# Splitting two blocks of the FFN activations where they are made instead of where they are multiplied

## The chip, the cores and the metric

The kernel runs on one core of one Trainium2 chip. The time is device microseconds of one launch: a median of 2877.29 us over three runs of the kernel before (2876.45 to 2877.64). One more execution was profiled, and every row below is from it. The engines are PE (TensorE, with PEld for its weight loads), DVE (VectorE), ACT (ScalarE), POOL (GpSimd) and SP (SyncE, which here only issues DMAs). Each engine works through its own instructions in order.

## The reference

Two layers, each a mixer (a gated delta net in layer 0, retention in layer 1) and a convolutional FFN, each followed by a residual sum and a layer norm. Sequence 1024, width 1024, FFN width 2816, all in float32. The change concerns the FFN alone:

```python
def conv_ffn(h, w_up, conv_w, conv_b, w_down):
    gate, up = jnp.split(h @ w_up, 2, axis=-1)
    gate = causal_dwconv(gate, conv_w) + conv_b
    return (jax.nn.silu(gate) * up) @ w_down

for i in range(DEPTH):
    ...
    y = conv_ffn(x * (1.0 + sc2) + sh2, ffn_up[i], ffn_conv_w[i], ffn_conv_b[i], ffn_down[i])
    x = layer_norm(DN_ALPHA * x + (1.0 + g2) * y, ln_g[i, 1], ln_b[i, 1])
```

Below, `o` is the product `silu(gate) * up`, the left factor of the down projection.

## The kernel before, in words

**Products in two parts.** A float32 factor x is written as a high part (x rounded to fp32r) and a low part (x minus the high part, again fp32r). A product of two such factors is three matmuls: low by high, high by low, high by high. `split` (L88 to L90) makes the parts: ACT copies x into the high part (L89), then DVE (or POOL, where a table says so) subtracts it from x (L90). So the subtraction waits for ACT each time.

**Blocks.** Both FFN projections use a Strassen-Winograd scheme on 2 by 2 blocks, with seven block products for eight. The left factor of the down projection is needed as seven blocks, in the order of `ABLK`: 11, 12, 22 (plain quarters of `o`) and S1 to S4 (sums and differences of quarters). Quarter 21 is used only inside the sums.

**The up stage** (`strassen`). There are 22 items of two units of 128 features (four quarters: two units by two halves of the sequence), taken as 11 pairs: a gate item and then an up item with the same pair number `fp`. An item is seven products of 12 matmuls of 512 columns (`wino`): a11, a12, s1, s2, s4, s3, a22, where s1 to s4 are weight sums that DVE forms into PSUM (L1350). Every weight block is split into a tile `wb` by ACT and DVE before PE can use it. An item's weights are two 512 KB loads, L1361 (a11, a12) and L1362 (a21, a22), into two buffers of the tag `wr`; a load waits until the last reader of the item before has left its buffer, which for L1362 is the split of a22. Results leave through `sink`: the gate's four quarters are convolved (`conv_q`: ACT L1734, DVE L1739 twice, ACT L1740), the up's four quarters are multiplied into `o` by DVE (L1762) in the order of quarters 0, 1, 3, 2. After quarter 3, block 22 is stored; after quarter 2, POOL forms S1, S2, S4 and S3 one after another (L1770; for pair 0 it is DVE), and each is stored. The stores (L1751) are SP's, 256 KB each, to a DRAM tensor `ad` with seven blocks a pair.

Besides that, the up stage carries other work a piece at a time: columns or rows of the condition's modulation (`bg_ada`, DVE L237 and L239; in layer 0 over nearly the whole stage, in layer 1 over its first pairs) and a gain of the residual on POOL (L411, L412).

**The down projection** (`proj_gen`). It has seven products p of 11 steps j; the left block of p is 11, 12, S1, S2, S4, S3, 22 in that order. A step is 12 matmuls. For a step, SP loads the left block from `ad` into `ar` (tag `qkv`, 20 buffers) and, three steps ahead, the weight block `Br` or `Bw`; both are split, into `ab` and `bb`. `ab` and `bb` take their buffers from a ring of the tags `wl`, `wr`, `wh` with two buffers each, two taken a step, so a buffer comes free when the step three before has ended. In layer 1 (`final`) a longer ring with the eight buffers of `hTb` is used, and the last six left blocks of product 22 lie in `hTb`; in layer 0 the last four lie in `qkv`. Between the steps, DVE finishes earlier products (`f1` to `f7`, `finish`, `norm`). In layer 0 the eight blocks of the next input are also built during the S3 product; in layer 1 the rows are normalised and written to the output.

**What sets the order.** The kernel is traced in the order of the code. A scheduler that runs a timeline of its own then orders each engine's instructions and hands out the buffers; `after(...)` adds an order on one engine. On the chip that order is fixed: an instruction that waits holds up all behind it on its engine.

The names that count below: `store` and `up_start` (L1750 to L1774), `ops` (L1481), `ablk_of` (L1425), and the tag `t2`, three buffers of 128 by 512, which the up stage uses for one copy an item (L1389).

Of the kernel before, what the change touches and what calls it, by code (L numbers as in the profile page):

```python
# [9 lines left out]
F32 = mybir.dt.float32  # L10
# [5 lines left out]
P = 128  # L16
# [3 lines left out]
HALF = 512  # L20
# [4 lines left out]
NF = F // P  # L25
HP = 3000
ABLK = ("11", "12", "22", "S1", "S2", "S3", "S4")
ALPHA = 4.0 ** 0.25
BAL = {"r11": 0, "r12": 0, "r22": 0, "rS1": 0, "rS2": 0, "rS3": 0, "rS4": 0, "rw21": 0, "rwT1": 0, "rwT2": 0, "rwT3": 0, "rwT4": 0, "rn": 0, "rh": 1, "011": 0, "012": 0, "022": 0, "0S1": 0, "0S2": 0, "0S3": 0, "0S4": 0, "0w21": 0, "0wT1": 0, "0wT2": 0, "0wT3": 0, "0wT4": 0, "0n": 1, "0h": 0, "f11": 0, "f12": 0, "f22": 0, "fS1": 0, "fS2": 0, "fS3": 0, "fS4": 0, "fw21": 0, "fwT1": 0, "fwT2": 0, "fwT3": 0, "fwT4": 0, "fn": 1, "fh": 0, "gw": 99, "gh": 0, "gn": 3, "b1": 0, "b2": 0, "b3": 0, "b4": 0, "bT": 0, "ba": 0, "rw11": 0, "rw22": 0, "0w11": 0, "0w22": 0, "fw11": 0, "fw22": 0}
LN_EPS = 1e-5  # L30
# [3 lines left out]
def trunk_kernel(ctx: ExitStack, tc, A):  # L34
# [53 lines left out]
    def split(dst_h, dst_l, src, eng=dve):  # L88
        anchor["sp"] = act.activation(dst_h, src, AF.Copy)  # L89
        eng.tensor_tensor(dst_l, src, dst_h, ALU.subtract)  # L90
# [1339 lines left out]
            return raw  # L1430
        return ablk

    def proj_gen(nj, ablk, wsrc, slots, xsrc, G, final, ln_next, tag, ltags, dst, key, mm=pe.matmul, gate=None):
        bal = {nm: BAL[ltags[4] + nm] for nm in ABLK + ("w11", "w21", "w22", "wT1", "wT2", "wT3", "wT4", "n", "h")}
        pa = [tl("aux", [P, 2, HALF], name="pa") for _ in range(4)]
        p1 = [pa[t // 2][:, t % 2] for t in range(4)]
# [27 lines left out]
        def bblk(bn, j):  # L1464
            if bn in ("11", "22"):
                return {"11": C, "22": X}[bn][j]
            if bn == "21":
                return R[bn, j]
            if bn == "T1":
                dve.tensor_tensor(C[j], R[bn, j], C[j], ALU.subtract)  # L1470
                return C[j]
            if bn == "T2":
                dve.tensor_tensor(C[j], X[j], C[j], ALU.subtract)
                return C[j]
            x, y = (R[bn, j], C[j]) if bn == "T4" else (C[j], R[bn, j])
            dve.tensor_tensor(R[bn, j], x, y, ALU.subtract)
            return R[bn, j]
# [1 line left out]
        nst = [0]  # L1479

        def ops(an, bn, j, early):  # L1481
            ra, rb = ablk(an, j), bblk(bn, j)
            n = nst[0]
            nst[0] += 1
            last = an == "22"
            ring = ("wl", "wr", "wh")
            at = ltags[0] if last and j >= nj - ltags[3] else ("wl", "hTb", "wr")[n % 3] if early else ring[2 * n % 3]
            wt = ltags[1] if last and j >= nj - ltags[2] else ("wh", "hTb", "hTb")[n % 3] if early else ring[(2 * n + 1) % 3]
            a = two(at, F32R, "ab")
            split(a[0], a[1], ra, pool if j < bal[an] else dve)  # L1490
            w = two(wt, F32R, "bb")
            split(w[0], w[1], rb, pool if j < bal["w" + bn] else dve)
            return a, w
# [188 lines left out]
    def layer_tail(i, mix, wout, xsrc, x_mid, x_out, ln_next, final):  # L1682
# [24 lines left out]
        cw = vcol(f"ffn_conv{i}")  # L1707
        cb = vcol(f"ffn_convb{i}")
        ad = dr.tile([NF // 2, 7, P, HALF], F32, tag=f"ad{i}", name=f"ad{i}")
        up = A["ffn_up"][i]  # L1710

        late = []

        def pair_items(fp):
            g, o = [], {}

            def gate_start():
                g.extend(tl("lane", [P, D], name="g") for _ in range(2))

                def gate(q, a, b):  # L1720
                    dst = g[q // 2][:, hs(q % 2)]
                    if b is None:
                        act.activation(dst, a, AF.Copy)
                    else:
                        dve.tensor_tensor(dst, a, b, ALU.add)
                return gate

            def conv_q(q):
                f, hf = 2 * fp + q // 2, q % 2
                gv = g[q // 2]  # L1730
                w = cw[:, 3 * f:3 * f + 3]
                t = tl("qkv", [P, HALF], name="o")
                with after("sp") if fp == 0 else nullcontext():
                    act.activation(t, gv[:, hs(hf)], AF.Copy, scale=w[:, 2:3])  # L1734
                for j in (1, 2):
                    c0 = HALF if hf else j
                    c1 = HALF * (hf + 1)
                    tv = t[:, c0 - HALF * hf:]
                    dve.scalar_tensor_tensor(tv, gv[:, c0 - j:c1 - j], w[:, 2 - j:3 - j], tv, ALU.mult, ALU.add)  # L1739
                act.activation(t, t, AF.Silu, bias=cb[:, f:f + 1])  # L1740
                o[q] = t

            def conv():
                for q in (1, 3, 0, 2) if fp == 0 else range(4):
                    if fp < 2:
                        late.append(lambda q=q: conv_q(q))
                    else:
                        conv_q(q)

            def store(nm, q):  # L1750
                sp.dma_start(ad[fp, ABLK.index(nm)], o[q])  # L1751

            def up_start():
                seen = []

                def gated(q, a, b):
                    while q not in o:
                        late.pop(0)()
                    c = a
                    if b is not None:  # L1760
                        dve.tensor_tensor(c, a, b, ALU.add)
                    dve.tensor_tensor(o[q], o[q], c, ALU.mult)  # L1762
                    if q != 1:
                        store({0: "11", 2: "12", 3: "22"}[q], q)
                    seen.append(q)
                    if len(seen) == 4:
                        for d, x, y, op, nm in ((1, 1, 3, ALU.add, "S1"), (0, 1, 0, ALU.subtract, "S2"),
                                                (2, 2, 0, ALU.subtract, "S4"), (3, 3, 0, ALU.subtract, "S3")):
                            def one(d=d, x=x, y=y, op=op, nm=nm):
                                (dve if fp == 0 else pool).tensor_tensor(o[d], o[x], o[y], op)  # L1770
                                store(nm, d)
                            if fp == 0:
                                late.append(one)
                            else:  # L1774
                                one()
                return gated

            return [(up[4 * fp], up[4 * fp + 2], gate_start, conv), (up[4 * fp + 1], up[4 * fp + 3], up_start, None)]
# [5 lines left out]
        if not final:  # L1784
            wnext_up.append(A["ret_wg"][2])
        gb2 = gain_rows(3, ("mid", i), "hTb") if final else None
        return proj_st(proj_gen(NF // 2, ablk_of(ad, "qkv"), A["ffn_down"][i], slots, xg[i + 1], rows[i, 5],
                       (gb2, x_out) if final else None, ln_next, "hTb", ("hTb", "hTa", 8, 6, "f") if final else ("qkv", "hTa", 8, 4, "0"), x_out, ("out", i)))

    g1 = two("auh", F32, "g1")  # L1790
    for nh in range(2):
# [384 lines left out]
```

## Time and profile before

| | |
|---|---|
| median of three runs | 2877.29 us |
| the profiled execution | 2872.01 us, its span 2870.2 us |
| granted TensorE clock | 0.994 |
| PE, PEld busy | 97%, 79% of the span |
| DVE, ACT, POOL busy | 76%, 45%, 17% of the span |
| DMA | 465.30 MB, a mean of 162 GB/s |
| stores `ad<-o`, loads `ar<-ad` | 154 each of 256 KB, 2.3 us and 4.7 us to landing (median) |

PE leaves the up stage at 1157.8 us in layer 0 and at 2644.5 us in layer 1; the down projections follow it. Their matmuls end near 1380 us and at 2855.97 us.

In a row of grouped instructions stand the line, the engine, the operation, out<-in by the program's names, the shape, the count, then the busy time and the mean of one in ns, then the idle time of the engine just before them and what ended it. In a row of the timeline stand the start, the duration, the engine, the line and the tiles, and in brackets the idle time before it with its releaser. In a row of windows stand the window, its length, each engine's busy time and count, the granted clock, the DMA engines' busy share and their GB/s. Matmuls are pipelined: one of 512 columns is shown with some 390 ns, and they start 0.23 us apart.

### The profile page before, as it was taken

What the parts mean: (1) busy time and instruction counts of PE and PEld (TensorE: products, weight loads), DVE (VectorE), ACT (ScalarE), POOL (GpSimd) and SP (SyncE); (2) the same over time, 40 slices, a digit from 0 to 9 for tenths busy, and PEclk for the clock granted to TensorE, in tenths of its full rate; (3) what the DMA queues carried; (4) which work ended last, traced back from release to release, by engine and by line L of the source; (5) the groups of instructions that cost most, each with busy time, mean ns of one, the idle gap of its engine ahead of it and who ended that gap; (6) DMA issues with size and microseconds to landing.
All of it is one profiled execution on the core that took longest, in us unless ns stands there. A gap on an engine that the chain in (4) does not pass through costs nothing.

```text
span 2870.2 us, 38920 instructions
## 1 busy us (share of the span) xinstructions
PE 2783.2 (97%) x13594; PEld 2276.5 (79%) x13594; DVE 2180.0 (76%) x3874; ACT 1296.7 (45%) x2387; POOL 486.9 (17%) x513
## 2 busy tenths in 40 slices
PE   8999999999999999999999999999999999999997
PEld 6778878887788878887888887777777788888886
DVE  6787778676788888778687656666788887777869
ACT  4664465344644444545433342222344644445443
POOL 0311321000023222000000002343201033322001
PEclk9999999999999999999999999999999999999999
DMA  7233242174255554945343354665754253444843
GB/s 279 85 99 122 92 133 96 64 246 153 99 180 172 195 182 167 337 133 172 129 147 131 116 198 156 198 208 155 258 203 147 74 194 132 143 139 164 319 148 118
DMA packets 252884, 465.30 MB, mean 162 GB/s; under 512 B 24144, under 2 KB 77776, under 8 KB 252688
## 3 DMA queue, kind: packets, MB, share of 16 engines
q1 hardware_dynamic: 218560, 408.02, 42.8%
q10 hardware_dynamic: 31488, 46.15, 4.4%
q0 software_dynamic: 2640, 8.65, 0.8%
q8 instruction: 107, 1.75, 0.2%
q14 instruction: 89, 0.73, 0.1%
HBM read 346.86 MB, written 115.87 MB: 161 GB/s over the span
## 4 chain that ended last, share of the span: by engine, by line
PE 60%; DVE 20%; DMA 8%; ACT 5%; issue 5%; POOL 1%; SPq 0%; ACTq 0%; DVEq 0%; POOLq 0%
PE acc L716 11%; PE acc L1296 5%; PE acc L1591 5%; PE sc L716 4%; PE acc L110 4%; PE acc L111 4%; PE acc L112 4%; PE sc L1296 3%; PE mm L716 2%; DVE o L1739 2%; DVE wb L90 2%; DMA mvw<-in_ada_w 2%; DMA wr<-in_ffn_up 2%; DVE mm L1350 2%; DVE ada L239 2%
## 5 line engine op out<-in xcount | busy, mean ns | idle before, releaser
L716 PE MATMUL acc<-hT,wh 128*128 128x512 f32 x960 | 298.3, 392 | 0.0
L1591 PE MATMUL acc<-bb,ab 128*128 128x512 f32 x984 | 230.9, 393 | 5.6 <-DVE bb L90 2.4
L89 ACT ACTIVATE ab<-ar 128x512 fp32r<-128x512 f32 x210 | 131.1, 630 | 218.9 <-PE mm L303 53.6
L1591 PEld LDWEIGHTS acc<-bb,ab 128*128 128x128 f32 x984 | 184.3, 189 | 47.3 <-DVE bb L90 3.2
L716 PEld LDWEIGHTS acc<-hT,wh 128*128 128x128 f32 x960 | 181.6, 189 | 35.3
L1296 PE MATMUL acc<-T,wb 128*128 128x512 f32 x840 | 202.0, 389 | 0.4 <-DVE wb L90 0.4
L89 ACT ACTIVATE wb<-mm 128x512 fp32r<-128x512 f32 x216 | 124.4, 597 | 167.3 <-DVE mm L1350 152.2
L90 DVE TENSOR_TENSOR ab<-ar,ab 128x512 fp32r<-128x512 f32 x210 | 145.8, 702 | 71.2 <-ACT ab L89 70.9
L716 PE MATMUL acc<-hT,wl 128*128 128x512 f32 x480 | 196.1, 409 | 2.5 <-ACT sq L509 2.5
L1296 PEld LDWEIGHTS acc<-T,wb 128*128 128x128 f32 x840 | 157.5, 188 | 33.8 <-ACT o L1740 1.2
L90 DVE TENSOR_TENSOR wl<-wr,wh 128x1024 fp32r<-128x1024 f32 x98 | 122.5, 1250 | 74.3 <-ACT wh L89 73.8
L89 ACT ACTIVATE wh<-wr 128x1024 fp32r<-128x1024 f32 x98 | 103.8, 1060 | 137.9 <-PE acc L716 54.3
L90 DVE TENSOR_TENSOR wb<-wr,wb 128x512 fp32r<-128x512 f32 x162 | 116.3, 719 | 64.2 <-ACT wb L89 64.1
L1770 POOL TENSOR_TENSOR o<-o 128x512 f32<-128x512 f32 x80 | 112.3, 1412 | 267.4 <-ACT pc L1366 173.1
L1739 DVE SCALAR_TENSOR_TENSOR o<-g,vc,o 128x512 f32<-128x512 f32 (+2 forms) x176 | 147.1, 845 | 8.6 <-ACT o L1734 7.3
L90 DVE TENSOR_TENSOR wb<-mm,wb 128x512 fp32r<-128x512 f32 x216 | 144.4, 681 | 7.4 <-ACT wb L89 7.4
L89 ACT ACTIVATE wb<-wr 128x512 fp32r<-128x512 f32 x162 | 101.1, 626 | 93.8 <-PE acc L1296 27.1
L1350 DVE TENSOR_TENSOR mm<-wr 128x512 f32<-128x512 f32 x108 | 85.7, 794 | 69.9 <-DMA wr<-in_ffn_up 56.8
L716 PE MATMUL acc<-wh,hT 128*128 128x512 f32 x384 | 134.8, 413 | 2.1 <-DVE vv L90 2.1
L1366 ACT ACTIVATE pc<-acc 128x512 f32<-128x512 f32 x143 | 84.4, 590 | 108.6 <-PE acc L1296 63.2
L239 DVE SCALAR_TENSOR_TENSOR ada<-mvw,e,ada 128x512 f32<-128x512 f32 x140 | 105.4, 753 | 26.6 <-DMA mvw<-in_ada_w 26.3
L110 PE MATMUL acc<-T,wb 128*128 128x512 f32 x292 | 114.4, 392 | 3.5 <-DVE wb L90 3.4
(675 smaller groups left out, 7348.1 us busy)
## 6 DMA issues: line engine op xcount, KB each, us to landing
wr<-in_ffn_up SPq DMA_DIRECT2D x92, 512.0 KB, 3.9
mvw<-in_ada_w SPq DMA_DIRECT2D x80, 512.0 KB, 4.4
ad<-o SPq DMA_DIRECT2D x154, 256.0 KB, 2.3
ar<-ad SPq DMA_DIRECT2D x154, 256.0 KB, 4.7
Br<-in_ffn_down SPq DMA_DIRECT2D x88, 256.0 KB, 5.2
wr<-in_ret_wv SPq DMA_DIRECT2D x32, 512.0 KB, 3.6
ar<-od SPq DMA_DIRECT2D x56, 256.0 KB, 5.0
wr<-in_gdn_wqkv SPq DMA_DIRECT2D x24, 512.0 KB, 3.5
```

Of the source, the lines that this page charges most:

```text
L89: anchor["sp"] = act.activation(dst_h, src, AF.Copy)
L90: eng.tensor_tensor(dst_l, src, dst_h, ALU.subtract)
L110: mm(acc, wl[:, k], hl[0], start=first, stop=False)
L111: mm(acc, wh[:, k], hl[1], start=False, stop=False)
L112: mm(acc, wh[:, k], hl[0], start=False, stop=last)
L239: dve.scalar_tensor_tensor(a, wr[:, kk], e[:, k:k + 1], a, ALU.mult, ALU.add)
L716: pq(pe.matmul(out, lhsT, rhs, start=start, stop=stop), cost or COST[out.shape[-1]])
L1296: return pe.matmul(*a, skip_group_check=True, **kw)
L1350: dve.tensor_tensor(t, x, y, op)
L1591: return pe.matmul(*args, skip_group_check=True, **kw)
L1739: dve.scalar_tensor_tensor(tv, gv[:, c0 - j:c1 - j], w[:, 2 - j:3 - j], tv, ALU.mult, ALU.add)
L1770: (dve if fp == 0 else pool).tensor_tensor(o[d], o[x], o[y], op)
```

## The change

For blocks 22 and S3 of both layers, `store` makes the two parts at once: ACT copies the block into a high part, DVE subtracts for a low part, both in tiles of the tag `t2`, and SP stores both to a new DRAM tensor `ah` in place of the one store to `ad`. In the down projection, the steps of products S3 and 22 load the two parts straight into the ring buffer `ab`, in two loads, and do not split the left block. The other five blocks are as before, and so is every matmul.

Per layer there are 22 such blocks, 44 in all: 44 splits (an ACT copy and a DVE subtraction) move from the down projection to the up stage, 44 stores of 256 KB become 88, and 44 loads become 88.

```diff
+HL = ("22", "S3")
...
-    def proj_gen(nj, ablk, wsrc, slots, xsrc, G, final, ln_next, tag, ltags, dst, key, mm=pe.matmul, gate=None):
+    def proj_gen(nj, ablk, wsrc, slots, xsrc, G, final, ln_next, tag, ltags, dst, key, mm=pe.matmul, gate=None, hlblk=None):
...
         def ops(an, bn, j, early):
-            ra, rb = ablk(an, j), bblk(bn, j)
+            pre = hlblk is not None and an in HL
+            ra, rb = None if pre else ablk(an, j), bblk(bn, j)
...
             a = two(at, F32R, "ab")
-            split(a[0], a[1], ra, pool if j < bal[an] else dve)
+            if pre:
+                for i in range(2):
+                    anchor["w"] = anchor["a"] = sp.dma_start(a[i].bitcast(F32), hlblk[j, HL.index(an), i])
+            else:
+                split(a[0], a[1], ra, pool if j < bal[an] else dve)
...
         ad = dr.tile([NF // 2, 7, P, HALF], F32, tag=f"ad{i}", name=f"ad{i}")
+        ah = dr.tile([NF // 2, 2, 2, P, HALF], F32, tag=f"ah{i}", name=f"ah{i}")
...
             def store(nm, q):
-                sp.dma_start(ad[fp, ABLK.index(nm)], o[q])
+                if nm not in HL:
+                    sp.dma_start(ad[fp, ABLK.index(nm)], o[q])
+                    return
+                hl = [tl("t2", [P, HALF], F32R, name="oh") for _ in range(2)]
+                act.activation(hl[0], o[q], AF.Copy)
+                dve.tensor_tensor(hl[1], o[q], hl[0], ALU.subtract)
+                for i in range(2):
+                    sp.dma_start(ah[fp, HL.index(nm), i], hl[i].bitcast(F32))
```

The call of `proj_gen` in `layer_tail` passes `hlblk=ah`; the retention's output projection does not, and is unchanged.

2 lines of the change are left out of this document (1 added, 1 removed).

## The prediction

> **What bounds the kernel now.** I read the totals first, then windows by stage, then the waits of a stage, then the timelines of its engines where a wait sits.
>
> ```profile
> PE 2783.2 (97%) x13594; PEld 2276.5 (79%) x13594; DVE 2180.0 (76%) x3874; ACT 1296.7 (45%) x2387; POOL 486.9 (17%) x513
> 787.00:1142.50 355.50, 351.63 (x1553) 287.39 (x1552) 300.08 (x462) 168.91 (x338) 104.64 (x84) 1.00 0.54 183
> 2290.00:2606.00 316.00, 315.48 (x1384) 259.26 (x1384) 247.52 (x365) 145.50 (x246) 98.89 (x79) 1.00 0.44 148
> ...
> 1320.00:1338.00 18.00, 18.00 (x84) 14.81 (x84) 15.91 (x36) 15.04 (x24) 2.63 (x3) 1.00 0.87 304
> ...
> 2820.00:2857.00 37.00, 35.07 (x153) 28.05 (x151) 37.00 (x72) 11.51 (x20) 6.38 (x4) 1.00 0.15 57
> 2857.00:2870.20 13.20, 0.00 (x0) 0.00 (x0) 9.98 (x22) 1.92 (x3) 3.05 (x2) 0.61 0.41 159
> ```
>
> The first row is the page's, the others are windows: layer 0's up stage (nine pairs of 39.5 us), layer 1's (eight), the middle of layer 0's S3 product, the kernel's last PE work, and what follows it. PE is the bound almost everywhere, so a split taken off DVE is worth nothing where PE is full. It counts in the last 50 us, where DVE is 100% busy and PE ends 14 us before the span does. And the up stage of layer 0 is not as free as 84% of DVE looks:
>
> ```profile
> PE acc L110 <- DVE wb L90: 3.4, 4, 1.2
> DVE mm L1350 <- DMA wr<-in_ffn_up: 24.2, 10, 3.6
> ```
>
> These are its waits by engine: PE already waits for DVE's weight splits, and DVE waits once a pair for a weight load. One pair, from one such stall to the next, on DVE, PE, POOL and SP:
>
> ```profile
> 904.86 1.29 DVE L1725 TENSOR_TENSOR g<-acc,pc 128x512 f32<-128x512 f32 x2 [1.27 <-ACT pc L1366]
> 906.07 1.28 DVE L90 TENSOR_TENSOR wb<-mm,wb 128x512 fp32r<-128x512 f32 x2
> 906.80 0.50 PE L110 MATMUL acc<-T,wb 128*128 128x512 f32 x1 [1.21 <-DVE wb L90]
> 924.61 5.62 POOL L1770 TENSOR_TENSOR o<-o 128x512 f32<-128x512 f32 x4
> 924.67 0.68 DVE L1762 TENSOR_TENSOR o<-o,sc 128x512 f32<-128x512 f32 x1
> 929.86 1.70 DVE L1739 SCALAR_TENSOR_TENSOR o<-g,vc,o 128x511 f32<-128x511 f32 x2 [0.24 <-ACT o L1734]
> 930.25 0.32 SPq L1751 DMA_DIRECT2D ad<-o  x1
> 931.48 0.69 DVE L90 TENSOR_TENSOR wb<-wr,wb 128x512 fp32r<-128x512 f32 x1
> 932.19 0.33 SPq L1362 DMA_DIRECT2D wr<-in_ffn_up  x1
> 933.41 0.69 DVE L90 TENSOR_TENSOR wb<-wr,wb 128x512 fp32r<-128x512 f32 x1 [1.25 <-ACT wb L89]
> 936.79 0.70 DVE L1350 TENSOR_TENSOR mm<-wr 128x512 f32<-128x512 f32 x1 [2.68 <-DMA wr<-in_ffn_up]
> ```
>
> Read it as a loop. From 904.86 to 932.16 DVE has hardly a gap. Its last job there, the split of a22, frees the weight buffer; SP issues the next load at 932.19; it lands at 936.8; then a chain of DVE and ACT work leads to the next weight split that PE needs, some 9 us later. In this pair and in about half of the others PE arrives first. So what is put on DVE between 905 and 932 moves the load, and PE's next stall, by its full length; what falls in the gaps at 932 to 937 is free.
>
> **The change, part by part.** All matmuls stay.
>
> *Up stage, layer 0.* Per pair two ACT copies, two DVE subtractions and two more stores are added.
>
> ```profile
> L90 DVE TENSOR_TENSOR wb<-mm,wb 128x512 fp32r<-128x512 f32 x8 | 5.3, 681 | 0.0
> L90 DVE TENSOR_TENSOR wb<-wr,wb 128x512 fp32r<-128x512 f32 x6 | 5.2, 870 | 1.3 <-ACT wb L89 1.3
> L89 ACT ACTIVATE ab<-ar 128x512 fp32r<-128x512 f32 x210 | 131.1, 630 | 218.9 <-PE mm L303 53.6 <-PE mm L1591 42.2 <-PE acc L1591 39.9
> ```
>
> The first two rows are DVE's splits in that pair: 0.68 us with one input in PSUM, 0.87 us with both in SBUF, as the new ones have them. Block 22's subtraction becomes ready with the multiplication just before 924, in the dense stretch: +0.8 us on the loop. S3's becomes ready when POOL's chain ends at 930.2, plus 0.63 us of ACT: about 931, within half a microsecond of a22's split. Behind that split it falls in the gap and costs nothing, except that its second store, if it stands ahead of L1362 on SP, delays the load by about 0.8 us; in front of it, 0.8 us to 1.5 us. So the load comes later by 0.8 to 2.3 us, and I take 1.1. Less the 0.3 us of slack that the pairs without a stall have, that is 0.8 us on nine pairs: **+7 us**, bounds 0 (DVE fits it all into gaps) and +18. ACT has room (169 us of 355). The extra 512 KB a pair is 13 GB/s on 183. The three `t2` buffers hold at most one copy and one pair of parts at a time, as the parts of 22 leave some 6 us before those of S3 are made; a store takes about 2 us.
>
> The Trainium skill speaks against the move here: page "SBUF — State Buffer", section "Who interferes with whom", says that a DVE instruction with two SBUF inputs contends with a GpSimd instruction that reads SBUF, and the later one waits until the earlier is done. The rows agree in kind (870 ns against 681) but not in full, since not each of them meets a POOL instruction. By the rule alone block 22's subtraction would wait for a rest of one of four POOL instructions; what that makes is the last rival.
>
> *Up stage, layer 1.* Less other work is mixed in, and the split that PE waits for is earlier:
>
> ```profile
> 2552.54 0.68 DVE L90 TENSOR_TENSOR wb<-mm,wb 128x512 fp32r<-128x512 f32 x1
> 2554.03 0.39 PE L110 MATMUL acc<-T,wb 128*128 128x512 f32 x1
> ```
>
> It ends 0.81 us before its use, and PE lost 0.5 us in 316. The same 1.1 us leaves 0.3 us in some pairs: **+1 us**, bounds 0 and +8.
>
> *Down projection, layer 1.*
>
> ```profile
> L90 DVE TENSOR_TENSOR ab<-ar,ab 128x512 fp32r<-128x512 f32 x18 | 12.0, 679 | 0.0
> ...
> 2841.55 0.96 PE L1591 MATMUL acc<-bb,ab 128*128 128x512 f32 x3 [0.66 <-DVE ab L90]
> 2842.76 3.47 PE L1591 MATMUL acc<-bb,ab 128*128 128x512 f32 x14 [0.24 <-DVE ab L90]
> 2843.78 12.19 PE L1591 MATMUL acc<-bb,ab 128*128 128x512 f32 x53
> ...
> 2846.83 0.69 DVE L1517 TENSOR_TENSOR acc<-acc,rowb 128x512 f32<-128x512 f32 x1
> 2857.02 0.69 DVE L1517 TENSOR_TENSOR acc<-acc,rowb 128x512 f32<-128x512 f32 x1
> 2866.36 0.69 DVE L1540 TENSOR_TENSOR xt<-xt,rowb 128x512 f32<-128x512 f32 x1
> ```
>
> The first row groups DVE's window 2796 to 2843: 18 left-block splits, and since two of 0.68 take 1.28 (row 906.07), one costs 0.60 in a full queue: 10.8 us, all of which go. DVE has no gap from there to the end. The last group of four accumulators is 72 matmuls at 0.23 us, so the first is done 12.3 us before PE's end at 2855.97, at 2843.7; DVE begins it at 2846.83, behind by 3.1 us. With the backlog gone it follows PE: each accumulator costs DVE 4.6 us (seven operations of 0.6 to 0.66 and small ones) against PE's 4.1, so the fourth starts at PE's end plus about 1 us less what PE gains (0.9 us of stalls), and its own chain with nothing of others in between takes some 6 us instead of the 10 from 2857.02 to 2867.05. That gives an end of DVE at about 2862.5: **-4.5 us**, bounds -6.5 and 0 (the scheduler keeps the order in which the accumulators' steps are mixed). The loads of the parts have a ring some six steps deep there and DMA is at 0.15.
>
> *Down projection, layer 0.* PE stalls near its end would go; the loads are the risk.
>
> ```profile
> 1317.49 0.63 ACT L89 ACTIVATE ab<-ar 128x512 fp32r<-128x512 f32 x1 [5.83 <-PE acc L1591]
> 1320.26 0.63 ACT L89 ACTIVATE ab<-ar 128x512 fp32r<-128x512 f32 x1 [1.61 <-PE acc L1591]
> ...
> 1354.36 0.66 PE L282 MATMUL mm<-cst,xt 128*128 128x128 f32 x4 [0.82 <-ACT t L284]
> 1355.56 1.65 PE L1591 MATMUL acc<-bb,ab 128*128 128x512 f32 x6 [0.54 <-DVE ab L90]
> ...
> DMA to landing us min/median/max: 2.6/3.4/6.3
> ```
>
> A left split starts when PE leaves the buffer, about every 2.75 us, two steps (5.5 us) ahead of use. Now two loads start there instead. The last row is the left loads of 1310 to 1342: 3.4 us for one, about 4.2 for two, in time; but 1320 to 1338 already moves 304 GB/s at a share of 0.87, thus 349 at most. Six or seven more loads of 262 KB make 401: 18 us of traffic become 20.7. The queue behind SP's waiting load is the weight load for three steps on, which has room. I take +2.5 for the DMA and -1.5 for the two stalls: **+1 us**, bounds -2 and +6.
>
> The sum is 7 + 1 - 4.5 + 1 = +4.5 us on the profiled execution's 2872.01 (span 2870.2 and 1.8 around it). The median of the runs is 5.3 us above that execution, and the difference goes onto the median: 2881.8, say **2882**. About 0.2% (5.8 us, so 2871.5 to 2883.0) is what a measurement can tell from no change; the forecast is a loss inside it.
>
> **The rivals.**
>
> *The up stage absorbs it* (not slower). The loop has 5.4 us of gaps a pair (1.27, 0.24, 1.25 and 2.68), and the scheduler may put both subtractions there. Against: block 22's is ready 8 us before the first gap of size and, traced earlier, goes first. Then 0 + 0 - 4.5 - 1.5 = -6: **2871**.
>
> *The in-order wait on POOL* (slower). If the scheduler's clock has POOL done earlier than the chip, S3's copy and subtraction stand well before a22's split, and ACT and DVE stand idle until POOL is done. It decides from the point where POOL's end at 930.2 plus ACT's 0.6 is later than DVE's turn; at 1.5 us a pair over the slack on nine pairs in layer 0 (+13.5) and 0.7 on eight in layer 1, whose slack is 0.8 (+5.6), the sum is 13.5 + 5.6 - 4.5 + 1 = +15.6: **2893**. Against: SP's order of stores and weight loads, laid down by the same scheduler, fits POOL's real end (S3's store at 930.25, 1.9 us ahead of L1362).
>
> *Loads late in layer 0's S3 and 22 products.* With a landing of 8 us for the pair, three steps take 11 us for 8.2, nine steps long: +8.4, less the 1.5: +7 in place of +1, the rest as in the sum: **2888**.
>
> *Contention with POOL.* Each of block 22's subtractions waits out one POOL instruction of 1.4 us: 1.4 us on nine pairs, about 0.5 on eight: +17 on the sum: **2898**. The page above has the rule; the 870 ns bear out a seventh of it.
>
> **How the numbers follow.** Forecast 0.42 (its own range 2877 to 2888; no change 0.25, slower 0.17); absorbed 0.30 (2867 to 2876; faster 0.17, no change 0.13); wait on POOL 0.16, late loads 0.08, contention 0.04, all slower. Together faster 0.17, no change 0.38, slower 0.45: the likeliest time is inside the bound, while the rivals' mass lies beyond it. The range 2870 to 2893 cuts off the ends of the first and the last of these.
>
> **What would show it.** In the new profile, layer 0's up pairs: PE's stalls for `wb` L90 at up items of 1 to 2 us in nearly each pair (right), none (absorbed), 3 us with DVE idle behind POOL (wait on POOL). Layer 1's last accumulator: L1517 within 1 us of PE's end and the span's end some 9 to 10 us after PE's instead of 14. Layer 0's S3 product: PE waiting for `ah` loads, or not. The forecast is wrong if the up stage's length in layer 0 moves by under 2 us or over 14, or if the end keeps its 14 us.

## The result and the profile after

The changed kernel took 2887.09 us (median of six runs, 2882.72 to 2893.75), the kernel before 2876.40 us beside it (2874.78 to 2877.64): ratio 1.0034, 95% interval 1.0023 to 1.0044, a loss of about 10 us. The forecast was 2882.0, with 2870 to 2893 as its range. The direction and the range hold. The size does not: I had forecast a loss of 4.5 us, inside what a measurement can tell from no change, and it is more than twice that and clear of it. Of the terms, two were missed, and the mechanisms of three rivals that I had given little chance are there, at part of their size.

The profiled execution of after is the slowest of its six (2893.75 us, span 2892.0), that of before lies below its median (2872.01). So I compare stage by stage. Windows of the kernel before, cut at the first and last matmul of layer 0's up and down stages, of layer 1's, and at the end of PE (columns: stretch, length, busy time of PE, PEld, DVE, ACT, POOL, clock, DMA share, GB/s):

```profile
763.00:1157.60 394.60, 389.24 (x1715) 317.40 (x1714) 334.38 (x516) 190.53 (x374) 104.64 (x84) 1.00 0.51 173
1157.80:1377.60 219.80, 216.00 (x958) 177.67 (x957) 172.92 (x285) 111.15 (x191) 11.94 (x11) 0.99 0.62 213
2257.70:2644.30 386.60, 385.08 (x1687) 315.69 (x1686) 306.59 (x456) 183.30 (x310) 106.10 (x84) 1.00 0.43 144
2644.50:2856.00 211.50, 210.53 (x925) 173.00 (x923) 174.88 (x293) 98.65 (x174) 15.94 (x10) 1.00 0.60 207
2856.00:2870.20 14.20, 0.00 (x0) 0.00 (x0) 10.98 (x24) 2.92 (x4) 3.05 (x2) 0.64 0.38 148
```

The same of the changed kernel:

```profile
770.30:1168.50 398.20, 389.88 (x1715) 317.37 (x1714) 348.36 (x536) 198.13 (x394) 108.56 (x84) 1.00 0.55 185
1168.70:1396.00 227.30, 218.53 (x958) 178.93 (x957) 159.38 (x261) 101.49 (x171) 9.70 (x10) 0.98 0.66 232
2278.30:2668.20 389.90, 386.01 (x1687) 315.47 (x1686) 322.34 (x476) 191.89 (x330) 107.69 (x84) 1.00 0.45 157
2668.40:2880.40 212.00, 210.88 (x925) 172.95 (x923) 167.35 (x279) 89.74 (x155) 14.78 (x10) 1.00 0.69 240
2880.40:2892.00 11.60, 0.03 (x1) 0.00 (x0) 7.70 (x18) 1.62 (x2) 1.84 (x2) 0.67 0.29 113
```

DVE's work moved as intended: 14 to 16 us more in each up stage, 13.5 and 7.5 us less in the down stages. The losses stand in layer 0: 3.6 us in its up stage and 7.5 us in its down stage, with 3.3 us in layer 1's up stage; the end gives back 2.6 us. The rest of the 21.8 us between the two spans (some 9.5 us) lies in stretches whose code the change doesn't touch. These together took between 1641 and 1656 us in the fourteen profiles of this study, so a difference of that size between two single executions says nothing.

### The profile page after: what moved, and what is told of

It is laid out like the page before. It is cut to its first block, busy times and chain, and to the rows that moved or that the text cites. A ratio compares the mean times of both kernels' runs of the same rounds, so it can differ in the third digit from the quotient of the medians.

```text
span 2892.0 us, 39009 instructions
## 1 busy us (share of the span) xinstructions
PE 2792.8 (97%) x13594; PEld 2281.5 (79%) x13594; DVE 2185.8 (76%) x3874; ACT 1293.2 (45%) x2387; POOL 485.1 (17%) x513
## 5 line engine op out<-in xcount | busy, mean ns | idle before, releaser
L91 DVE TENSOR_TENSOR ab<-ar,ab 128x512 fp32r<-128x512 f32 x166 | 118.5, 720 | 81.0 <-ACT ab L90 80.9
L90 ACT ACTIVATE ab<-ar 128x512 fp32r<-128x512 f32 x166 | 103.6, 628 | 162.0 <-PE mm L304 48.9
L1351 DVE TENSOR_TENSOR mm<-wr 128x512 f32<-128x512 f32 x108 | 78.7, 729 | 54.4 <-DMA wr<-in_ffn_up 41.6
L111 PE MATMUL acc<-T,wb 128*128 128x512 f32 x292 | 114.4, 392 | 3.5 <-DVE wb L91 3.5
```

Source lines behind the costliest of these rows:

```text
L111: mm(acc, wl[:, k], hl[0], start=first, stop=False)
L1351: dve.tensor_tensor(t, x, y, op)
```

## Where the time went

**Layer 0's up stage: the loop is there.** Waits of PE and of DVE in the changed kernel, that stage (us in total, times, longest; the line numbers are one higher than before up to about L1480, and up to 14 higher behind):

```profile
PE acc L111 <- DVE wb L91: 3.5, 4, 1.8
PE sc L111 <- DVE wb L91: 1.4, 1, 1.4
...
PE acc L1297 <- ACT pc L1367: 1.2, 2, 0.7
PE sc L1297 <- ACT pc L1367: 0.9, 2, 0.7
...
DVE mm L1351 <- DMA wr<-in_ffn_up: 13.6, 8, 2.2
...
DVE oh L1763 <- ACT oh L1762: 6.4, 8, 1.3
```

PE's waits for weight splits at these products went from 3.8 us (3.4 and 0.4) to 4.9, and DVE's idle time for the weight load from 24.2 to 13.6: nearly half of the gap that I had called free has been filled. The two rows in the middle are the larger part of what PE waits longer: it stands 2.1 us for `pc`, a copy by ACT, where it was 0.3 us before. The last row is new: DVE stands 0.8 us per pair behind ACT's copy of S3. One pair shows how these hang together (DVE, POOL, ACT, PE and SP of the changed kernel):

```profile
931.84 1.18 DVE L1763 TENSOR_TENSOR oh<-o,oh 128x512 fp32r<-128x512 f32 x1
932.54 4.59 POOL L1784 TENSOR_TENSOR o<-o 128x512 f32<-128x512 f32 x3
...
935.91 0.63 ACT L1762 ACTIVATE oh<-o 128x512 fp32r<-128x512 f32 x1 [1.59 <-POOL o L1784]
936.57 1.10 DVE L1763 TENSOR_TENSOR oh<-o,oh 128x512 fp32r<-128x512 f32 x1 [1.25 <-ACT oh L1762]
...
937.60 0.68 DVE L1732 TENSOR_TENSOR g<-acc,pc 128x512 f32<-128x512 f32 x1
...
938.31 0.72 ACT L1741 ACTIVATE o<-g,vc 128x512 f32<-128x512 f32 x1 [1.28 <-DVE g L1732]
938.94 0.58 ACT L1367 ACTIVATE pc<-sc 128x512 f32<-128x512 f32 x1
...
939.57 0.97 PE L1297 MATMUL sc<-22_6965,wb 128*128 128x512 f32 x3 [0.68 <-ACT pc L1367]
...
940.52 0.69 DVE L91 TENSOR_TENSOR wb<-wr,wb 128x512 fp32r<-128x512 f32 x1
...
941.23 0.33 SPq L1363 DMA_DIRECT2D wr<-in_ffn_up  x1
```

The first row is block 22's subtraction, the fourth S3's. S3's copy on ACT waits for POOL, and S3's subtraction waits for the copy. Both engines hold back what is queued behind: DVE's next step, then ACT's two, and PE at the end of the chain. The a22 split comes only 4 us later (3.1 us in most pairs), so S3's subtraction stands ahead of it and not in the gap behind. This is the in-order wait on POOL of my rivals, at half its size.

**Layer 0's down stage: the loads come late.** PE's wait for loads there, in the changed kernel:

```profile
PE acc L1597 <- DMA ab<-ah: 5.5, 2, 3.9
```

The two runs of matmuls behind these waits, on PE:

```profile
1348.02 4.15 PE L1597 MATMUL acc<-bb,ab 128*128 128x512 f32 x10 [1.65 <-DMA ab<-ah]
1375.03 4.35 PE L1597 MATMUL acc<-bb,ab 128*128 128x512 f32 x11 [3.88 <-DMA ab<-ah]
```

And windows around them:

```profile
1345.80:1348.20 2.40, 0.75 (x5) 0.52 (x6) 0.00 (x0) 2.40 (x5) 0.00 (x0) 1.00 0.99 369
1348.20:1351.60 3.40, 3.40 (x9) 2.67 (x10) 2.50 (x4) 0.36 (x1) 0.00 (x0) 0.52 1.00 348
...
1375.20:1378.60 3.40, 3.40 (x10) 2.64 (x10) 2.91 (x5) 1.26 (x2) 0.00 (x0) 0.56 1.02 354
```

PE waits for `ah` twice. Behind each wait its granted clock is about half for 3.4 us (the column ahead of the DMA share), so 9 or 10 matmuls pass instead of 15, at 0.23 us each: these two waits cost 1.2 to 1.4 us more than themselves. (The profile of before has one such stretch in this stage too, behind a wait of 2.4 us for a weight split.) The DMA share beside them is 0.99 to 1.02: there is no room. The loads of the last 66 us of this stage (issues: count, KB each, median us to landing) and that stretch as a window, first of before:

```profile
ar<-ad SPq DMA_DIRECT2D x12, 256.0 KB, 3.4
```
```profile
1311.00:1377.00 66.00, 62.20 (x280) 50.56 (x279) 60.37 (x111) 38.63 (x64) 5.81 (x7) 0.97 0.53 180
```

The same of the changed kernel:

```profile
ab<-ah SPq DMA_DIRECT2D x33, 256.0 KB, 5.3
```
```profile
1330.00:1396.00 66.00, 59.38 (x259) 47.76 (x258) 44.69 (x81) 28.60 (x43) 2.74 (x5) 0.95 0.84 295
```

12 left loads with 3.4 us to landing became 33 with 5.3, and 180 GB/s became 295. The loads have also lost their lead. Before, they ran ahead into the buffers of `ar`; now SP can issue them only when the ring of `ab` comes free. The left loads of this stage, before and in the changed kernel (count, ns to issue one, first and last start):

```profile
L1429 SPq DMA_DIRECT2D ar<-ad x72: 319/320/1147, 1158.3 to 1340.4; - x72
L1494 SPq DMA_DIRECT2D ab<-ah x44: 319/323/1016, 1308.2 to 1379.0; - x44
```

The last of them was issued 37 us ahead of the stage's end before, and 17 us ahead of it now. Of the two waits, the first ended with a load that took 9.5 us, the longest of all. The second ended with one that took 7.2 us and whose pair was issued at 1367.25, 3.9 us ahead of PE's need at 1371.15: SP had stood 1.6 us behind another load that waited for DVE.

**The end: the backlog is gone, half of the gain too.** DVE behind layer 1's last accumulators in the changed kernel:

```profile
2868.18 0.70 DVE L1523 TENSOR_TENSOR acc<-acc,rowb 128x512 f32<-128x512 f32 x1 [0.82 <-PE acc L1597]
...
2880.54 0.67 DVE L1523 TENSOR_TENSOR acc<-acc,rowb 128x512 f32<-128x512 f32 x1
...
2883.77 0.67 DVE L1545 TENSOR_TENSOR xt<-xt,rowb 128x512 f32<-128x512 f32 x1
...
2888.10 0.69 DVE L1546 TENSOR_TENSOR xt<-xt,rowb 128x512 f32<-128x512 f32 x1
```

DVE now waits for PE (0.82 us) and begins the last accumulator 0.14 us after PE's end at 2880.40. But from there its steps take 8.25 us to the end of the last row, not 6, because the third accumulator's last steps (2883.77 is one) still stand among them.

## The experiments

The experiments were timed against the kernel before on the same chip. The stage lengths, each from one profile, are from the start of the stage's first matmul to that of its last; a star marks a stage whose code is that of before:

| kernel | ratio to before, interval | up 0 | down 0 | up 1 | down 1 | PE's end to end |
|---|---|---|---|---|---|---|
| before | | 394.6* | 219.4* | 386.6* | 211.1* | 14.3* |
| after | 1.0034, 1.0023 to 1.0044 | 398.2 | 226.9 | 389.9 | 211.6 | 11.5 |
| after, second profile | 1.0033, 1.0021 to 1.0044 | 401.9 | 223.8 | 388.4 | 210.9 | 11.6 |
| layer 1 only | 1.0006, 0.9994 to 1.0017 | 396.1* | 218.6* | 387.7 | 211.7 | 11.3 |
| layer 0 only | 1.0020, 1.0004 to 1.0035 | 400.7 | 219.0 | 387.7* | 211.8* | 14.0* |
| two plain copies | 1.0019, 1.0008 to 1.0030 | 400.5 | 220.7 | 387.4 | 211.6 | 11.6 |
| up stages only | 1.0020, 1.0009 to 1.0030 | 398.1 | 222.8* | 388.7 | 211.6* | 14.3* |
| one load | 0.9994, 0.9985 to 1.0003 | 398.1 | 216.0 | 386.8 | 209.3 | 11.3 |
| subtraction on POOL | 1.0087, 1.0073 to 1.0100 | 410.2 | 222.4 | 395.2 | 211.2 | 11.6 |
| last six steps | 1.0003, 0.9994 to 1.0012 | 397.7* | 220.4* | 387.7 | 213.1 | 12.7 |
| stores from ACT | 1.0014, 1.0004 to 1.0025 | 398.8 | 220.3 | 387.3 | 210.7 | 11.6 |
| splits alone | 1.0029, 1.0019 to 1.0039 | 402.6 | 219.1* | 388.7 | 211.0* | 14.3* |
| block 22 alone | 1.0029, 1.0018 to 1.0040 | 400.6 | 220.0 | 390.6 | 210.4 | 11.4 |
| block S3 alone | 1.0040, 1.0025 to 1.0056 | 403.0 | 223.5 | 387.9 | 213.7 | 12.6 |

The starred entries show how far one profile of the same code stands from another: 394.6 to 397.7, 218.6 to 222.8, 386.6 to 387.7, 211.0 to 211.8, 14.0 to 14.3. The changed code varies as much or more: layer 0's up stage took 398.1 to 401.9 us in the four profiles with the changed kernel's instructions there (after, after again, layer 0 only, one load), and its down stage 219.0 to 226.9 us in the three with the same instructions in the same order (after, after again, layer 0 only).

**One layer at a time.**

```diff
-                if nm not in HL:
+                if nm not in HL or not final:      # layer 1 only; "or final" for layer 0 only
...
-... hlblk=ah)
+... hlblk=ah if final else None)                    # and the reverse
```

> The change in layer 1 alone (layer 0 splits its left blocks in the down projection as before). Reading of the two profiles: layer 1's up stage costs +3.3 us, its down projection and tail give -2.3 us: +1 us against the kernel before, -2 to +4. Rival, the loss is spread evenly over both layers' up stages: +5 us. Rival, the loss is noise of the clock in stages that are not changed: 0 us here and in all the others. In the profile: the time from PE's end to the span's end 11 to 12 us (14.3 before).

> The change in layer 0 alone. Reading of the two profiles: up stage +3.6 us, down projection +7.5 us: +11 us, +7 to +14. Rival, an even spread over the layers' up stages: +5 us. In the profile: PE waits for loads of the parts in the S3 and 22 products of layer 0, 4 to 6 us in two or three waits, and DMA at a share of 0.95 around them; the end as before (14 us after PE's).

Layer 1 alone is no loss that can be measured (2878.57 against 2877.51 us), as expected; layer 0 alone loses 5.8 us (1.0020), less than my 7 to 14. Its down stage took 219.0 us, with 1.0 us of waits for `ah` where I had expected 4 to 6, so 226.9 us is not what this code always takes. Together 1.0026, which agrees with 1.0034 within the intervals. So layer 0 carries the loss.

**Two plain copies.** The block is stored twice and both copies are loaded; the copy on ACT and the subtraction on DVE are left out, so that both parts are the block itself.

```diff
-                hl = [tl("t2", [P, HALF], F32R, name="oh") for _ in range(2)]
-                act.activation(hl[0], o[q], AF.Copy)
-                dve.tensor_tensor(hl[1], o[q], hl[0], ALU.subtract)
                 for i in range(2):
-                    sp.dma_start(ah[fp, HL.index(nm), i], hl[i].bitcast(F32))
+                    sp.dma_start(ah[fp, HL.index(nm), i], o[q])
```

> Left out: the two splits in the up stages; the unsplit block is stored twice, as if it were both parts, so the products of blocks 22 and S3 come out wrong. All stores and loads of the change stay. Theory late loads (the loss is mostly DMA in layer 0's down projection): +7.5 - 2.3 = +5 us against before, about 5 to 7 us under the changed kernel. Rival (the loss is the splits in the up stages, with DVE waiting for POOL): -2 to -4 us, the tail's gain alone.

The sum came as expected, but it lies in the wrong stage for my reasoning: the up stage took 400.5 us without any added DVE work. **Up stages only**, the down projections as before:

```diff
             def store(nm, q):
-                if nm not in HL:
-                    sp.dma_start(ad[fp, ABLK.index(nm)], o[q])
-                    return
+                sp.dma_start(ad[fp, ABLK.index(nm)], o[q])
+                if nm not in HL:
+                    return
...
-... hlblk=ah)
+... hlblk=None)
```

> The splits and stores of the parts in the up stages as in the change, and the unsplit blocks stored too; the down projections read and split those as before, nobody reads the parts. So this is the up stages' price alone, with one more store a block. Theory late loads: +7 us (3.6 + 3.3). Rival (all of the loss and the tail's gain's worth more is in the up stages): +12 us. Rival (DVE hides the splits): 0 to +2 us.

1.0020, or 5.8 us: near the forecast for the up stages. In layer 0's up stage PE's waits for weight splits at L111 are down to 0.8 us here, but it waits 5.1 us for ACT's copies `pc`: the same work can reach PE on either way, by the order in which the scheduler lays it.

**Splits alone.** To take the stores out as well, the parts are made and neither stored nor used.

```diff
-                for i in range(2):
-                    sp.dma_start(ah[fp, HL.index(nm), i], hl[i].bitcast(F32))
```

> The kernel before plus the copies on ACT and the subtractions on DVE in the up stages; the parts are not stored and not used, the blocks are stored and loaded as before (the work is added, nothing of the result uses it). Theory A (DVE's subtractions, stretched beside POOL, are the up stages' loss): layer 0's up stage 398-399 us against 394.6-396.1 of the code before, layer 1's 388-389, ratio to before 1.0015. Theory B (the added stores are the loss, as with two plain copies, which gave 400.5): layer 0's up stage 395-396, ratio 1.000 to 1.0005.

It lost as much as the whole change, and layer 0's up stage took 402.6 us. Theory A holds, at more than it had expected, but with two plain copies that stage took 400.5 us by the stores alone. PE's longest sum of waits there is the one for weight splits at L111: 6.9 us with the splits alone, 5.5 us with two plain copies. The two reach the same wait on different ways. A pair's stall is what is left of this sum: the load's time to landing, plus the chain of DVE and ACT from landing to PE's first matmul, less the lead by which SP issued the load ahead of PE's need. One pair each of before, of the splits alone and of the changed kernel (issue, landing as the end of DVE's wait, PE's stall in brackets):

```profile
1050.20 0.33 SPq L1362 DMA_DIRECT2D wr<-in_ffn_up  x1
...
1055.59 0.70 DVE L1350 TENSOR_TENSOR mm<-wr 128x512 f32<-128x512 f32 x1 [3.14 <-DMA wr<-in_ffn_up]
...
1065.08 0.50 PE L110 MATMUL acc<-T,wb 128*128 128x512 f32 x1 [1.00 <-DVE wb L90]
```
```profile
976.89 0.33 SPq L1363 DMA_DIRECT2D wr<-in_ffn_up  x1
981.17 0.70 DVE L1351 TENSOR_TENSOR mm<-wr 128x512 f32<-128x512 f32 x1 [2.35 <-DMA wr<-in_ffn_up]
...
990.50 0.50 PE L111 MATMUL sc<-T,wb 128*128 128x512 f32 x1 [1.42 <-DVE wb L91]
```
```profile
1101.59 0.33 SPq L1363 DMA_DIRECT2D wr<-in_ffn_up  x1
1106.42 0.70 DVE L1351 TENSOR_TENSOR mm<-wr 128x512 f32<-128x512 f32 x1 [2.01 <-DMA wr<-in_ffn_up]
...
1115.27 0.50 PE L111 MATMUL sc<-T,wb 128*128 128x512 f32 x1 [1.45 <-DVE wb L91]
```

Before: lead 1065.08 - 1.00 - 1050.20 = 13.9, landing 5.4, chain 9.5. Splits alone: lead 12.2, landing 4.3, chain 9.3. Changed kernel: lead 12.2, landing 4.8, chain 8.9. Worked out in this way for the seven pairs of layer 0 from about 865 us on (means; the chain from the pairs with a stall):

| kernel | lead | landing | chain | PE's stalls in the seven pairs |
|---|---|---|---|---|
| before | 13.7 | 4.8 | 9.5 | 3.8 |
| layer 1 only (layer 0 as before) | 13.7 | 4.9 | 9.4 | 4.9 |
| last six steps (layer 0 as before) | 13.8 | 5.1 | 9.6 | 6.6 |
| two plain copies | 13.9 | 5.5 | 9.4 | 7.2 |
| splits alone | 12.5 | 4.4 | 9.4 | 9.2 |
| block S3 alone | 12.8 | 4.7 | 9.4 | 9.0 |
| block 22 alone | 13.6 | 5.0 | 9.6 | 7.4 |
| after | 12.3 | 4.6 | 8.4 | 4.9 |
| after, second profile | 12.7 | 4.8 | 8.8 | 5.6 |
| layer 0 only (layer 0 as after) | 12.3 | 4.8 | 8.5 | 6.5 |
| subtraction on POOL | 11.9 | 5.3 | 8.4 | 12.3 |

The splits take 1.2 us off the lead, which varied by 0.1 us in the three profiles of layer 0 as before. Two plain copies leave the lead and have a landing of 5.5 us, against 4.8 to 5.1. That the added stores make it longer is likely but not shown: the changed kernel has as many of them and lands in 4.6 to 4.8 us. With both, the lead is short too, yet the chain is 0.7 to 1.1 us shorter, since the scheduler laid DVE's steps behind the landing in another order. That takes back what the lead lost: the stalls of the changed code, 4.9 to 6.5 us, lie within those of layer 0 as before, 3.8 to 6.6. So the effects don't add, and what PE lost more in the changed kernel's stage is for the most part not in this loop but in its waits for ACT: 1.3 to 2.1 us in the four profiles of that code, 0 to 0.3 in the three of the code before.

**Subtraction on POOL.**

```diff
-                dve.tensor_tensor(hl[1], o[q], hl[0], ALU.subtract)
+                pool.tensor_tensor(hl[1], o[q], hl[0], ALU.subtract)
```

> The changed kernel with the two subtractions of a pair on POOL in place of DVE. Theory A (DVE's subtraction of 1.1 to 1.7 us, stretched by POOL's instruction beside it, delays the weight load): layer 0's up stage falls from 398-400 us to 395-396, the whole to about 2883 (ratio 1.002). Theory B (the added stores on SP's queue and their traffic delay the weight load, as in the run with two plain copies): layer 0's up stage stays at 398-401, the ratio at 1.003. If POOL's longer chain makes S3's block late, it is worse than the changed kernel: 402 and more.

The worst of all: 410.2 us, as expected for a longer chain on POOL. The lead is the shortest of the table, and DVE has a new wait for POOL (first row PE, second DVE):

```profile
PE acc L111 <- DVE wb L91: 7.3, 5, 2.6
...
DVE o L1746 <- POOL o L1784: 4.4, 6, 0.7
```

It doesn't tell A from B, as the move changes POOL more than it relieves DVE.

**Stores from ACT's queue.**

```diff
-                    sp.dma_start(ah[fp, HL.index(nm), i], hl[i].bitcast(F32))
+                    act.dma_start(ah[fp, HL.index(nm), i], hl[i].bitcast(F32))
```

> The changed kernel with the four part stores of a pair issued by ACT in place of SP. Theory B (part stores ahead of the weight load on SP's queue are what delays it): layer 0's up stage returns to 395-396 us, the whole to about 2883 (ratio 1.002). Theory A (the subtraction on DVE delays it): stays at 398-400, ratio 1.003. Theory C (ACT must wait in order for DVE's remainder before it issues the store, and ACT's weight copies come late): layer 0's up stage 402 or more, ratio 1.005.

The up stage stays at 398.8 us and the lead is 12.4: SP's queue isn't what delays the load. The whole is 1.0014, lower than the changed kernel's 1.0034 with intervals that just meet (1.0004 to 1.0025 and 1.0023 to 1.0044). In the profiles the difference stands in layer 0's down stage (220.3 against 226.9 and 223.8), whose code the edit doesn't touch, and that is within what this stage varies by (219.0 to 226.9). Whether the stores' queue is worth anything is open.

**One block at a time.**

```diff
-HL = ("22", "S3")
+HL = ("22",)          # block 22 alone; ("S3",) for S3 alone
```

> The changed kernel for block 22 alone, in both layers; S3 is stored and loaded as before. Theory (the double loads are late where they meet layer 0's other traffic, and each block's share of stores and splits costs the up stage its part): waits of PE for `ah` loads in layer 0's down stage only in the last eleven steps, 0.5 to 1.5 us, stage 218-220; end of PE to end of span 11.5 us as in the changed kernel, since the last stretch is block 22's; layer 0's up stage half the loss, 396-398; ratio 1.000 to 1.001. Rival (the loss hangs on block 22 alone): ratio 1.003 as in the changed kernel.

> The changed kernel for block S3 alone, in both layers; 22 is stored and loaded as before. Theory (S3's copy and subtraction fall into DVE's gap behind the split of a22, block 22's into the dense stretch ahead of the weight load): layer 0's up stage as before, 394-397 us, where block 22 alone had 400.6; in layer 0's down stage some late loads in S3's steps, 219-221 us; the end keeps 13.5 to 14.3 us, since the last eleven steps are block 22's; ratio 1.000 to 1.001. Rival (either block's added DVE work delays the weight load alike): up stage 398-401, ratio 1.002 to 1.003.

Both theories missed. Block 22 alone came out like its rival (1.0029, up stage 400.6), but block S3 alone lost as much (1.0040, 403.0), so the loss doesn't hang on block 22: either block costs the up stage what both cost (one profile each). S3, which I had put into DVE's gap for nothing, is no cheaper than block 22. (S3 alone also missed its down stage in layer 0, 223.5 us for 219 to 221, and its end, 12.6 us for 13.5 to 14.3.) DVE's wait for its copy in the whole stage:

```profile
DVE oh L1763 <- ACT oh L1762: 11.6, 8, 1.9
```

Without block 22's work ahead of it, DVE arrives earlier and waits longer: 1.45 us a pair. With block 22 alone the lead is 13.6 us and PE stalls for 7.4 us, not far from the 6.6 that one profile of layer 0 as before has; by what way that stage became longer is not shown.

**One load.**

```diff
-                for i in range(2):
-                    anchor["w"] = anchor["a"] = sp.dma_start(a[i].bitcast(F32), hlblk[j, HL.index(an), i])
+                anchor["w"] = anchor["a"] = sp.dma_start(a[0].bitcast(F32), hlblk[j, HL.index(an), 0])
+                a = (a[0], a[0])
```

> The changed kernel, but the down projections load only the copy of each of the two blocks and use it for both parts; the remainders are made and stored as in the changed kernel but not loaded (so the low part of these left blocks is left out of the computation). All matmuls stay. Theory (in layer 0's down projection the second load of a step is what makes PE wait and puts its clock down): layer 0's down stage returns from 226.9 us to 219-220, no waits of PE for `ah` loads, and the whole to about 2881 (ratio to before about 1.0015). Rival (the loss sits in the up stages, and the down stage's is chance of one execution): ratio stays at 1.003, 2886.

All of the loss went: 2874.32 us, 0.9994, with an interval of 0.9985 to 1.0003 that holds no change. Layer 0's down stage fell to 216.0 us, below every profile of before (218.6 to 222.8), layer 1's to 209.3. PE's wait in layer 0's down stage, and the window of its last 66 us:

```profile
PE acc L1597 <- DMA ab<-ah: 0.3, 1, 0.3
```
```profile
1316.00:1382.00 66.00, 64.30 (x297) 52.32 (x296) 55.51 (x102) 30.02 (x46) 4.67 (x7) 1.00 0.75 259
```

So taking the left splits off DVE is worth some 4 us in layer 0's down stage and 2 us in layer 1's. The second load costs 3 to 11 us in the first (219.0 to 226.9 us in the six profiles in which both blocks have two loads, a mean of 222.2, less 216.0) and about 2 us in the second. In the whole it is 1.0034 less 0.9994, or 11.5 us: the largest term of the change.

**The changed kernel once more**, without an edit.

> The changed kernel once more, for a second profile, since the first was of its slowest run. Theory (late loads cost PE waits in every execution, of a size that changes from run to run): `ah` waits of 1 to 3 us in layer 0's down stage in place of 5.5, stage 219-222 us in place of 226.9, layer 0's up stage again 398-400; ratio 1.003. Rival (226.9 us is what this kernel always takes there): stage 225-228 again.

PE's wait for loads in layer 0's down stage of this profile:

```profile
PE acc L1597 <- DMA ab<-ah: 3.9, 4, 2.5
```

Four waits of 3.9 us in place of two of 5.5, ratio again 1.0033. The stage took 223.8 us, between theory and rival, and the up stage 401.9, over the 398 to 400 that I expected. The late loads are no accident of one execution. Their size varies: in the other profiles with both loads (layer 0 only, two plain copies, POOL, stores from ACT) the same wait came to 1.0, 2.6, 2.3 and 2.7 us.

**The last six steps only**, as an attempt to keep the gain of the end alone: layer 1, block 22, pairs 5 to 10.

```diff
-                if nm not in HL:
+                if nm != "22" or not final or fp < NF // 2 - 6:
...
-            pre = hlblk is not None and an in HL
+            pre = hlblk is not None and an == "22" and j >= nj - 6
```

> The change for layer 1's block 22 alone and only its last six steps (pairs 5 to 10), which is the stretch in which DVE is full; all else as before. Theory (the gain of the end needs only DVE's backlog of the last 3 us removed): end of PE to end of span 11.5 to 12.5 us in place of 14.3, layer 1's up stage +0 to +1, the whole -2 us: ratio 0.9993. Rival (six splits in the up stage cost what the end gains, or the backlog has its source further ahead): ratio 1.000, end 13 to 14 us.

The end shortens by 1.6 us (12.7), but the down stage is longer (213.1 against 211.0 to 211.8): PE waits once for 2.0 us for a weight split there, and twice, 0.9 us together, for `ah`. Nothing is left (1.0003). None of these kernels does the whole computation in less time than the kernel before.

## Why the prediction was right, and where it was not

The table gives the terms. Measured are the means of the two profiles of the changed kernel, less the means of the starred profiles of the same stage; the last column takes in every other profile that has the changed kernel's instructions in the stage.

| stage | forecast | measured | with the other profiles |
|---|---|---|---|
| up stage, layer 0 | +7 | 400.05 - 396.13 = +3.9 | 399.7 - 396.1 = +3.6 |
| up stage, layer 1 | +1 | 389.15 - 387.15 = +2.0 | 388.2 - 387.2 = +1.0 |
| down, layer 0 | +1 | 225.35 - 220.06 = +5.3 | 223.2 - 220.1 = +3.2 |
| down and end, layer 1 | -4.5 | 211.25 - 211.38 and 11.55 - 14.23 = -2.8 | -2.7 |
| sum | +4.5 | +8.4 | +5.1 |

The medians say +10.7 and +11.0. The 2 to 6 us that are missing are less than the 15 us that unchanged stretches vary by, so the sum of single profiles can't be held against the medians. That the time fell into the range is partly luck: the up stage of layer 0 came out 3 us cheaper than forecast, which hid as much of what its down stage and the end cost more, and the measured 2887 stands at the upper edge of the forecast's own range, 2877 to 2888.

- *Up stage, layer 0.* "Moves the load, and PE's next stall, by its full length": shown with the splits alone. They took 1.2 us off the lead (forecast 1.1) and lengthened the stage by 6.5 us (402.6 less 396.1; forecast 7). In the changed kernel less than 4 us are left, because the chain behind the landing came out shorter, and about half of these are waits for ACT, which the forecast did not have; I had taken the order of DVE's other steps as fixed.
- *S3's place.* "About 931, within half a microsecond of a22's split": this step failed. S3's copy and subtraction stand 3 to 4 us ahead of that split and wait for POOL, 6.4 us over the stage. I had S3 ready when POOL's chain ends; in the pair shown the copy begins at 935.91 while POOL's run of four lasts until 937.13, so S3 was not the last of the four. It is the rival's mechanism, at 0.8 us a pair in place of the 1.5 that would have given 2893. My evidence against it, that S3's store stood 1.9 us ahead of the weight load on SP, was about SP, not about ACT and DVE.
- *Contention with POOL.* The forecast had 0.8 us for a subtraction; the eighteen of the nine pairs took 0.69 to 1.74 us, a mean of 1.15. So the two of a pair take 0.9 us more than they would undisturbed (0.68 each): the rival's mechanism is there, at two thirds of its 1.4 us, and for S3 as well as for block 22. With block 22 alone, one that began inside a run of four POOL instructions shows its kind (POOL's first instruction of the run by itself, and DVE's):

```profile
1051.49 1.30 POOL L1784 TENSOR_TENSOR o<-o 128x512 f32<-128x512 f32 x1
1051.93 1.42 DVE L1763 TENSOR_TENSOR oh<-o,oh 128x512 fp32r<-128x512 f32 x1
```

  It began 0.44 us into POOL's instruction and ended 0.56 us after it, so it got through when that one was done. The Trainium skill, page "SBUF — State Buffer", section "Who interferes with whom", says just that, and this trace agrees: the cost is about the rest of one instruction, here 0.86 us of which 0.74 show.
- *Up stage, layer 1.* +1.0 to +2.0 for +1, inside the bounds.
- *Down, layer 0.* This term failed in both of its parts, though its sum stayed inside the bounds. "About 4.2 for two, in time" was the step: single loads took 5.3 us in the median of the last 66 us and up to 9.5 us, and some pairs were issued less than the 5.5 us ahead that I had counted on. I had priced the traffic (20.7 us for 18) as if it were spread evenly, and gave late loads 0.08. The second load costs 6 us here in the mean of six profiles (3 to 11), where I had 2.5. Which of the traffic beside them makes the loads late was not tested. That rival's 2888 is what comes closest to the measured 2887, but by luck: its +7 for this stage is more than the +3.2 to +5.3 measured. I also took 349 GB/s as the most, where 369 passed at a share of 0.99; so it wasn't the rate that was misjudged, but the waiting. And the gain was mis-sized too: the freed DVE is worth about 4 us in this stage by the run with one load (forecast 1.5).
- *The end.* The backlog went as forecast: the last L1523 starts 0.14 us after PE's end ("within 1 us"). "Its own chain with nothing of others in between" failed: 8.25 us for 6, so PE's end to the end of the span is 11.5 us and not 9 to 10. The bound at 0 was there for this reason.

## What to carry to other kernels

Work that is taken off an engine where it has room to spare and turned into traffic has to be priced where that traffic lands: ask what else moves in the same 20 us, and not what the stage moves in the mean, and how far ahead of their use the new loads can be issued. For a load in a loop, write down its lead, its landing and the chain behind it; all three change with an edit, by the added work, by the added stores and by the order in which a scheduler lays the rest. And before a step is costed at nothing because it falls into a gap, check that its input is there ahead of its turn on an in-order engine.

## What the runs showed of the hardware

- A wait of PE can cost more than itself. After waits of 1.65 and 3.88 us for `ah` the granted clock was 0.52 and 0.56 for 3.4 us, in place of 1.00. In the 3.4 us ahead of these stretches PE was busy for 1.24 and 0.57 us, so it had stood idle for 2.2 us (a wait of 0.52 us for ACT is part of it) and for 2.8 us. The Trainium skill, page "TensorE: Matmul & The Clock Gate", section "HAM oscillation — how this bites in real kernels", asks for no idle gap of PE over about 3.4 us; the half clock agrees with that section, but here 2.2 us of idle time in two pieces were enough. Not each such wait does it: after one of 2.50 us in the second profile of the changed kernel (1374.84) the clock stayed at 1.00, and the seven stalls of 0.9 to 1.6 us in the up stage of the splits alone left the stage's clock at 1.00. What decides is not shown.
- The share of a whole stage hides what happens in a part of it: the DMA engines' 0.66 over layer 0's down stage is 0.84 over its last 66 us. There 256 KB left loads took 5.3 us in the median (5.6 at 0.87 with the stores from ACT), against 3.4 at 0.53 before. But they took 5.3 us at 0.75 with one load too, where PE waited only 0.3 us: the median doesn't tell whether a load is late.
- Stores that no one waits for are not free: with two more plain stores a pair and no added arithmetic, layer 0's up stage took 400.5 us in the one profile there is, where that of before took 394.6 to 397.7 in three.
